# One forward substitution for four heads, and spilled keys and queries, in a delta-net mixer

## The chip, the cores and the metric

The kernel runs on one core of a Trainium2 chip. The time is the device time of that core in microseconds, from launch to the end. The time before is the median of three runs, 2939.25 us (2938.39 to 2943.58). One more execution was recorded by the hardware profiler; it took 2940.32 us, and its span from the first to the last instruction is 2938.6 us.

## The reference

The program is a trunk of two layers over 1024 tokens of width 1024 in float32. Layer 0 has a gated delta-net mixer, layer 1 a retention mixer, and each is followed by a gated feed-forward block with a short convolution and by layer norms. The change touches the mixer of layer 0 alone. What it computes, with 8 heads, head width 128 and chunks of 64 tokens, is:

```python
proj = h @ w_in
qkv, z, a, bt = jnp.split(proj, ...)
qkv = jax.nn.silu(causal_dwconv(qkv, conv_w))          # 24 tiles of 128 features: q, k, v of 8 heads
q = _l2norm(q) * dk ** -0.5 ; k = _l2norm(k)
g = -exp(a_log) * softplus(a + dt_bias) ; gc = cumsum(g) ; decay = exp(gc_i - gc_j), i >= j
kk = where(strict, (k * beta) @ k.T * decay, 0)
sol = triangular_solve(kk + eye, [v * beta, k * beta * exp(gc)])   # unit lower triangular, per chunk and head
qk = where(causal, q @ k.T * decay, 0)
# scan over chunks: v_new = u - w @ S ; o = (q e^g) @ S + qk @ v_new ; S = S e^g_last + k^T v_new
o = rms_norm(o) * norm_w * silu(z) ; return o @ w_out
```

## The kernel before, in words

The kernel cuts the 1024 tokens into 8 chunks of 128 (NCH = 8; the delta rule gives the same result for any length of chunk). A "feature tile" is one 128-feature slice of q, k or v for all 1024 tokens; the code numbers them 0 to 7 (queries), 8 to 15 (keys, `GH + h` or `K + h`), 16 to 23 (values, `2 * GH + h` or `V + h`). It is kept as two half tiles of 512 tokens each in the tag `qkv`, which has 20 slots, so ten of the 24 feature tiles can be there at one time.

The delta-net stage is written as a set of Python generators, and a small planner, `run(todo)` (line 732), decides the order. Each generator has a priority (lower goes first) and yields either a delay, or a list of events to wait for, or a condition. The planner holds an estimated clock `clk[0]` that advances by a cost per matmul, and events carry an estimated time (`emit(name, lat)`, with the latencies in the table `LAT`). Whenever a generator may go on, the one with the smallest priority number does. The planner runs when the program is built. What it fixes on the chip is the order of all instructions of TensorE: each matmul is tied to the one before it (`pq`, line 703). Semaphores, the order on the other engines and the choice of buffers are made by the tile framework. `take(tag, n)` and `give(tag, n)` are the planner's own count of free buffers in `free`.

The generators before the change are:

- `gates()` (priority -1): decay and beta of all heads.
- `filler(items)` (priority 9, so it runs when nothing else may): projections with convolution. An item `("c", ti)` makes feature tile `ti`: a weight load, 48 matmuls of 512 columns, the convolution `conv_half` (ScalarE and VectorE, line 480), and for queries a sum of squares (`ssq_late`). It needs one slot of `qkv` for each half. An item `("z", ti)` makes an output gate, again 48 matmuls, and stores it to DRAM (`zd`); it needs no `qkv` slot. After each item one step of background work is done (`bg_step`, modulation vectors of later blocks).
- `t_path(p)` (p + 0.3) for pair p of heads: the decay matrices (`decay`, GpSimd, TensorE, VectorE, then Exp on ScalarE and a store to `Ld`), the key products (lines 851 to 868), and the forward substitution of the 32x32 diagonal blocks (lines 874 to 892). For the substitution the blocks of both heads are copied into `X`, of whose 32 columns 16 hold something (8 chunks of two heads) and 16 are set to zero, transposed in blocks of 32x32, and then 31 steps follow one another on VectorE, each a multiplication (line 883) and a subtraction (line 885). Pair p begins when pair p - 1 has passed the event `T0`.
- `t_chain(p)` (p + 0.2): the inverse blocks of 32 are joined to the whole inverse `R` with small matmuls; `prep(p)` (p + 0.25): transposed values and keys; `dt_half(p, q4)`: query-key products with decay.
- `scan(p, h)` (p + 0.0 and p + 0.05): the scan over 8 chunks, two heads side by side. At chunks 3 and 7 it starts `tail`, which writes the output of half the tokens and gives three `qkv` slots back.

Other buffers that matter: `aux` (4, one decay matrix `U` each), `lane` (4), `auh` (8 half tiles, for `R` and the second half of the query-key products), and `xT` (2, unused in this stage before).

The forward substitution before is

```python
for j in range(31):
    dve.tensor_tensor(tv, bc(Y[:, j + 1:, j], nj), bm(T[:, j, 0:nj], ni), ALU.mult)
    ts_ = T[:, j + 1:, 0:nj]
    dve.tensor_tensor(ts_, ts_, tv, ALU.subtract)
    yield LAT["fs"]
```

and the order of the filler is given by hand in `items`.

## Time and profile before

| What | us |
|---|---|
| median of three runs | 2939.25 |
| profiled execution | 2940.32 |
| its span | 2938.6 |
| TensorE matmul busy | 2810.8 (96%) |
| VectorE busy | 2210.9 (75%) |
| ScalarE busy | 1316.6 (45%) |
| GpSimd busy | 500.1 (17%) |
| planned delta-net stage, first filler matmul to last scan step | about 82 to 648 |

In the profile "PE" is TensorE (matmuls), "PEld" its weight loads, "DVE" VectorE, "ACT" ScalarE, "POOL" GpSimd and "SP" the engine that issues most DMAs. A row of a group reads: line, engine, operation, tile written <- tiles read, shape, count, then busy time, mean duration in ns, and the idle time before it with what ended it. A row of a stretch reads: from:to and length, then for each engine its busy time and the number of its instructions, then the granted TensorE clock (1.00 is full), the busy share of the DMA engines and GB/s. Matmuls overlap, so the duration of one (about 0.39 us for 512 columns) is longer than the step from one to the next.

### The profile page before, as it was taken

How to read it: one execution, taken by the hardware profiler on the slowest of the kernel's cores; microseconds unless marked ns; L12 is line 12 of the kernel's file. 1: busy time of each engine (PE TensorE's matmuls, PEld its weight loads, DVE VectorE, ACT ScalarE, POOL GpSimd, SP SyncE). 2: the span in 40 equal slices, each digit the busy share in tenths (PEclk: the TensorE clock that was granted, in tenths of full speed). 3: DMA queues.
4: the chain of work that ended last, by engine and by line, in shares of the span. 5: the costliest groups of instructions: out<-in, count | busy, mean ns of one | idle time of the engine just before them, and what ended most of it. 6: DMA issues, size and time to landing. Idle time of an engine off the chain costs nothing. (4 is left out here: it accounts for less than half of the span.)

```text
span 2938.6 us, 38910 instructions
## 1 busy us (share of the span) xinstructions
PE 2810.8 (96%) x13594; PEld 2291.5 (78%) x13594; DVE 2210.9 (75%) x3976; ACT 1316.6 (45%) x2413; POOL 500.1 (17%) x517
## 2 busy tenths in 40 slices
PE   8998899999999999999999999999999999999997
PEld 6887777887778888887778877777777788888886
DVE  6878787757688888858686665566789777777779
ACT  4745564444544444545333333221344544444543
POOL 0312221100013332000000021422202022331201
PEclk9999999999999999999999999999999999999999
DMA  7231222344245655745333364655573254434853
GB/s 289 84 119 62 80 79 80 112 161 158 86 154 175 215 186 173 290 148 188 133 136 112 129 233 139 209 166 163 188 243 134 77 190 143 134 125 157 295 186 115
DMA packets 248277, 459.01 MB, mean 156 GB/s; under 512 B 23633, under 2 KB 77265, under 8 KB 248081
## 3 DMA queue, kind: packets, MB, share of 16 engines
q1 hardware_dynamic: 215680, 404.87, 41.5%
q10 hardware_dynamic: 29760, 43.00, 4.0%
q0 software_dynamic: 2640, 8.65, 0.8%
q8 instruction: 107, 1.75, 0.2%
q14 instruction: 90, 0.73, 0.1%
HBM read 343.71 MB, written 112.72 MB: 155 GB/s over the span
## 5 line engine op out<-in xcount | busy, mean ns | idle before, releaser
L714 PE MATMUL acc<-hT,wh 128*128 128x512 f32 x960 | 301.9, 396 | 0.0
L1527 PE MATMUL acc<-bb,ab 128*128 128x512 f32 x984 | 232.9, 394 | 11.6 <-DVE bb L90 10.2
L1527 PEld LDWEIGHTS acc<-bb,ab 128*128 128x128 f32 x984 | 184.0, 189 | 54.7 <-DVE bb L90 14.6
L1229 PE MATMUL acc<-T,wb 128*128 128x512 f32 x840 | 204.0, 392 | 7.6 <-DVE wb L90 7.5
L714 PEld LDWEIGHTS acc<-hT,wh 128*128 128x128 f32 x960 | 183.7, 191 | 34.7
L89 ACT ACTIVATE ab<-ar 128x512 fp32r<-128x512 f32 x210 | 130.3, 625 | 167.8 <-PE mm L303 50.1
L714 PE MATMUL acc<-hT,wl 128*128 128x512 f32 x480 | 202.5, 422 | 0.0
L411 POOL TENSOR_TENSOR xg<-xg,gb 128x512 f32<-128x512 f32 x48 | 63.5, 1324 | 781.3 <-DMA xg<-xs 477.3
L90 DVE TENSOR_TENSOR ab<-ar,ab 128x512 fp32r<-128x512 f32 x210 | 146.5, 703 | 61.1 <-ACT ab L89 61.1
L1229 PEld LDWEIGHTS acc<-T,wb 128*128 128x128 f32 x840 | 156.4, 188 | 46.0 <-DVE wb L90 12.3
L90 DVE TENSOR_TENSOR wl<-wr,wh 128x1024 fp32r<-128x1024 f32 x98 | 122.4, 1249 | 75.6 <-ACT wh L89 75.4
L1692 POOL TENSOR_TENSOR o<-o 128x512 f32<-128x512 f32 x80 | 126.5, 1592 | 279.6 <-PE acc L112 185.3
L90 DVE TENSOR_TENSOR wb<-wr,wb 128x512 fp32r<-128x512 f32 x162 | 117.0, 727 | 73.2 <-ACT wb L89 71.8
L89 ACT ACTIVATE wh<-wr 128x1024 fp32r<-128x1024 f32 x98 | 103.9, 1061 | 152.0 <-PE acc L714 65.0
L90 DVE TENSOR_TENSOR wb<-mm,wb 128x512 fp32r<-128x512 f32 x216 | 145.6, 683 | 26.4 <-ACT wb L89 25.6
L1661 DVE SCALAR_TENSOR_TENSOR o<-g,vc,o 128x512 f32<-128x512 f32 (+2 forms) x176 | 153.0, 887 | 6.7 <-ACT o L1656 6.1
L89 ACT ACTIVATE wb<-mm 128x512 fp32r<-128x512 f32 x216 | 124.2, 595 | 72.1 <-DVE mm L1283 65.1
L89 ACT ACTIVATE wb<-wr 128x512 fp32r<-128x512 f32 x162 | 98.5, 627 | 107.1 <-DMA wr<-in_ffn_up 50.6
L1299 ACT ACTIVATE pc<-acc 128x512 f32<-128x512 f32 x143 | 84.6, 591 | 137.8 <-PE acc L1229 88.3
L714 PE MATMUL acc<-wh,hT 128*128 128x512 f32 x384 | 135.5, 417 | 1.0 <-DVE vv L90 1.0
L490 DVE SCALAR_TENSOR_TENSOR qkv<-raw,vc,qkv 128x512 f32<-128x512 f32 x144 | 111.6, 778 | 14.7 <-ACT qkv L488 13.8
L110 PE MATMUL acc<-T,wb 128*128 128x512 f32 x292 | 115.3, 395 | 5.4 <-DVE wb L90 5.4
(651 smaller groups left out, 7450.5 us busy)
## 6 DMA issues: line engine op xcount, KB each, us to landing
wr<-in_ffn_up SPq DMA_DIRECT2D x92, 512.0 KB, 4.3
mvw<-in_ada_w SPq DMA_DIRECT2D x80, 512.0 KB, 4.6
ad<-o SPq DMA_DIRECT2D x154, 256.0 KB, 3.0
ar<-ad SPq DMA_DIRECT2D x154, 256.0 KB, 3.7
Br<-in_ffn_down SPq DMA_DIRECT2D x88, 256.0 KB, 3.3
wr<-in_ret_wv SPq DMA_DIRECT2D x32, 512.0 KB, 4.2
ar<-od SPq DMA_DIRECT2D x56, 256.0 KB, 5.3
wr<-in_gdn_wqkv SPq DMA_DIRECT2D x24, 512.0 KB, 3.6
```

The source lines that it names most:

```text
L89: act.activation(dst_h, src, AF.Copy)
L90: eng.tensor_tensor(dst_l, src, dst_h, ALU.subtract)
L110: mm(acc, wl[:, k], hl[0], start=first, stop=False)
L411: pool.tensor_tensor(x, x, gb[0], ALU.mult)
L490: dve.scalar_tensor_tensor(oh, raw[:, 3 - j:515 - j], w[:, 3 - j:4 - j], oh, ALU.mult, ALU.add)
L714: pq(pe.matmul(out, lhsT, rhs, start=start, stop=stop), cost)
L1229: return pe.matmul(*a, skip_group_check=True, **kw)
L1299: act.activation(t, X, AF.Copy)
L1527: return pe.matmul(*args, skip_group_check=True, **kw)
L1661: dve.scalar_tensor_tensor(tv, gv[:, c0 - j:c1 - j], w[:, 2 - j:3 - j], tv, ALU.mult, ALU.add)
L1692: (dve if fp == 0 else pool).tensor_tensor(o[d], o[x], o[y], op)
```

## The change

Four things are done together, all in the delta-net stage.

1. `t_path` now serves a group g of four heads (two pairs): all 32 columns of `X` are used, and there are two forward substitutions of 31 steps instead of four. The decay matrices move out into a generator of their own, `t_decay(h)`, one per head, in order; those of heads 4 to 7 wait for the first tails of pair 0 (event `("M", 0)`). The decay matrices of heads 4 and 5 live in `xT`, those of the others in `aux`. `t_chain(p)` of both pairs of a group reads its half of the columns of the shared result; `RX` and `TX` are given back by the second one.
2. The substitution yields to the planner after every third step, for 4.4 instead of 1.3 after each.
3. `filler` has two more kinds of work. While the next item needs `qkv` slots and fewer than two are free, it first makes one of the feature tiles in the list `[q2, q3, k4, k5, k6, k7]` in an `xT` buffer and stores it to a new DRAM tensor `qd` (kind `"s"`), if an `xT` buffer is free, and otherwise a gate (`"z"`). A tile that was put away is loaded from `qd` when its item comes up and two slots are free.
4. The hand-written order of items is new: keys 2 and 3 come before the values, and the gates are no longer in the list but taken when the filler is short of slots, or at the end.

```diff
--- before.py
+++ after.py
@@ -764,7 +764,7 @@
     def q4s(q4):
         return slice(q4 * 4, (q4 + 1) * 4)
 
-    free = {"qkv": 20 - 2 * (len(first) - 1), "lane": 4, "aux": 4, "auh": 8, "t2": 3}
+    free = {"qkv": 20 - 2 * (len(first) - 1), "lane": 4, "aux": 4, "auh": 8, "t2": 3, "xT": 2}
 
     def take(tag, n):
         while free[tag] < n:
@@ -827,21 +827,23 @@
             dve.tensor_tensor(U[h][:, q4s(q4)], v4(pt), bm(mneg, 4), ALU.add)
             give("t2", 2)
 
-    def t_path(p):
-        heads = pairs[p]
-        yield after_ev(("T0", p - 1), ("g",))
-        yield from take("lane", 1)
-        X = tl("lane", [P, 32, 32], name="X")
-        pool.memset(X[:, :, 16:32], 0.0)
-        for h in heads:
-            yield from take("aux", 1)
-            U[h] = tl("aux", [P, NCH, P], name="U")
-            yield from decay(h)
-        for h in heads:
-            act.activation(flat(U[h]), flat(U[h]), AF.Exp)
-            sp.dma_start(Ld[h], flat(U[h]))
+    def uhome(h):
+        return "xT" if h in (4, 5) else "aux"
+
+    def t_decay(h):
+        yield after_ev(("g",), ("DD", h - 1), ("M", h // 4 - 1))
+        yield from take(uhome(h), 1)
+        U[h] = tl(uhome(h), [P, NCH, P], name="U")
+        yield from decay(h)
+        act.activation(flat(U[h]), flat(U[h]), AF.Exp)
+        sp.dma_start(Ld[h], flat(U[h]))
+        emit(("DD", h))
+
+    def t_path(g):
+        heads = pairs[2 * g] + pairs[2 * g + 1]
+        X = None
         for hh, h in enumerate(heads):
-            yield after_ev(("f", GH + h))
+            yield after_ev(("f", GH + h), ("DD", h))
             sk = tl("sm", [P, NCH], name="sk")
             cj[h] = tl("sm", [P, NCH], name="cj")
             ir[h] = tl("sm", [P, NCH], name="ir")
@@ -866,6 +868,10 @@
                     n = q4 * 4 + c
                     dve.scalar_tensor_tensor(U[h][:, n], pt[:, c * P:(c + 1) * P], cj[h][:, n:n + 1],
                                              U[h][:, n], ALU.mult, ALU.mult)
+            if X is None:
+                yield after_ev(("T0", 2 * g - 1))
+                yield from take("lane", 1)
+                X = tl("lane", [P, 32, 32], name="X")
             for b in range(4):
                 bs = slice(32 * b, 32 * b + 32)
                 act.activation(X[bs, :, hh * 8:hh * 8 + 8].rearrange("p i c -> p c i"), U[h][bs, :, bs], AF.Copy)
@@ -883,17 +889,18 @@
             dve.tensor_tensor(tv, bc(Y[:, j + 1:, j], nj), bm(T[:, j, 0:nj], ni), ALU.mult)
             ts_ = T[:, j + 1:, 0:nj]
             dve.tensor_tensor(ts_, ts_, tv, ALU.subtract)
-            yield LAT["fs"]
+            if j % 3 == 2:
+                yield LAT["fs"]
         RX = tl("lane", [P, 32, 32], name="RX")
         dve.transpose(flat(RX), flat(T))
         TP = tl("lane", [P, 32, 32], name="TP")
         act.activation(TP, T.rearrange("p i j -> p j i"), AF.Copy)
         TX = tl("lane", [P, 32, 32], name="TX")
         dve.transpose(flat(TX), flat(TP))
-        RTX[p] = (RX, TX)
+        RTX[g] = (RX, TX)
         give("lane", 1)
-        emit(("Tq", p))
-        emit(("T", p), LAT["T"])
+        emit(("Tq", g))
+        emit(("T", g), LAT["T"])
 
     def rx(h, n):
         return R[h][n // 4][:, n % 4 * P:n % 4 * P + P]
@@ -903,15 +910,16 @@
 
     def t_chain(p):
         heads = pairs[p]
-        yield after_ev(("T", p), ("Dt", p - 1))
-        RX, TX = RTX[p]
+        yield after_ev(("T", p // 2), ("Dt", p - 1))
+        RX, TX = RTX[p // 2]
+        cx = p % 2 * 16
         yield from take("auh", 4)
         yield from take("lane", 1)
         emit(("T0", p))
         T0 = tl("lane", [P, 2, NCH, 64], name="T0")
         lo, hi = slice(0, 64), slice(64, 128)
         for hh, h in enumerate(heads):
-            ch = slice(hh * 8, hh * 8 + 8)
+            ch = slice(cx + hh * 8, cx + hh * 8 + 8)
             pool.memset(T0[0:32, hh, :, 32:64], 0.0)
             for b in range(3):
                 bs = slice(32 * b, 32 * b + 32)
@@ -922,7 +930,7 @@
             for q4 in range(2):
                 Rv = v4(R[h][q4])
                 pool.memset(Rv, 0.0)
-                ch = slice(hh * 8 + q4 * 4, hh * 8 + q4 * 4 + 4)
+                ch = slice(cx + hh * 8 + q4 * 4, cx + hh * 8 + q4 * 4 + 4)
                 for b in range(4):
                     bs = slice(32 * b, 32 * b + 32)
                     src = RX[bs, :, ch].rearrange("p i c -> p c i")
@@ -930,7 +938,8 @@
                         act.activation(Rv[bs, :, bs], src, AF.Copy)
                     else:
                         pool.tensor_copy(Rv[bs, :, bs], src)
-        give("lane", 2)
+        if cx:
+            give("lane", 2)
         yield LAT["T0"]
         yield from take("t2", 1)
         pa = mm_tile()
@@ -985,7 +994,7 @@
 
     def prep(p):
         heads = pairs[p]
-        yield after_ev(("Tq", p), *[("f", 2 * GH + h) for h in heads])
+        yield after_ev(("Tq", p // 2), *[("f", 2 * GH + h) for h in heads])
         for q4 in range(2):
             for h in heads:
                 pt = mm_tile()
@@ -1007,12 +1016,12 @@
     def dt_half(p, q4):
         heads = pairs[p]
         if q4 == 0:
-            yield after_ev(("Tq", p), ("M", p - 1))
+            yield after_ev(("Tq", p // 2), ("M", p - 1))
             yield from take("lane", 1)
             t = tl("lane", [P, 2, HALF], name="DT")
             tiles = [t[:, 0], t[:, 1]]
         else:
-            yield after_ev(("Tq", p), ("S", p - 1))
+            yield after_ev(("Tq", p // 2), ("S", p - 1))
             yield from take("auh", 2)
             emit(("Dt", p))
             tiles = [tl("auh", [P, HALF], name="DT") for _ in range(2)]
@@ -1076,7 +1085,7 @@
                 yield [(0.5, tail(p, h, n // 4))]
             if n < NCH - 1:
                 yield LAT["s3"]
-        give("aux", 1)
+        give(uhome(h), 1)
         emit(("Sh", h))
         if all(("Sh", g) in events for g in pairs[p]):
             emit(("S", p))
@@ -1119,10 +1128,31 @@
     def ssq_late(ti):
         yield LAT["ssq"]
         ssq_tile(ti, ptr)
-        emit(("f", ti), 1.0)
-
-    def filler(items):
-        for kind, ti in items:
+        if ti in away:
+            give("xT", 1)
+        else:
+            emit(("f", ti), 1.0)
+
+    qd = dr.tile([3 * GH, P, S], F32, tag="qd", name="qd")
+    away = []
+
+    def filler(items, zs, qs):
+        items = list(items)
+        while items or zs:
+            short = not items or (items[0][0] == "c" and free["qkv"] < 2)
+            if short and qs and items and free["xT"]:
+                kind, ti = "s", qs.pop(0)
+            elif short and zs:
+                kind, ti = "z", zs.pop(0)
+            else:
+                kind, ti = items.pop(0)
+            if kind == "c" and ti in away:
+                yield from take("qkv", 2)
+                feats[ti] = two("qkv", F32, "qkv")
+                for half in range(2):
+                    sp.dma_start(feats[ti][half], qd[ti, :, hs(half)])
+                emit(("f", ti), LAT["ld"])
+                continue
             if kind == "h":
                 if ti > 1:
                     acc = acc_tile()
@@ -1135,10 +1165,14 @@
                 else:
                     emit(("f", first[ti]), LAT["fv"])
                 continue
-            w = load_w(A["gdn_wqkv" if kind == "c" else "gdn_wz"][ti])
+            w = load_w(A["gdn_wz" if kind == "z" else "gdn_wqkv"][ti])
             prev = None
-            if kind == "c":
+            if kind != "z":
                 feats[ti] = []
+            if kind == "s":
+                yield from take("xT", 1)
+                away.append(ti)
+                oq = two("xT", F32, "oq")
             for half in range(2):
                 if kind == "c":
                     yield from take("qkv", 1)
@@ -1146,35 +1180,40 @@
                 for k in range(KT):
                     mm3(acc, w, k, hT[half][k], k == 0, k == KT - 1, pm)
                     yield 0.0
-                if kind == "c":
-                    feats[ti].append(tl("qkv", [P, HALF], name="qkv"))
+                if kind != "z":
+                    feats[ti].append(tl("qkv", [P, HALF], name="qkv") if kind == "c" else oq[half])
                     prev = conv_half(ti, acc, half, feats[ti], prev)
+                    if kind == "s":
+                        act.dma_start(qd[ti, :, hs(half)], feats[ti][half])
                 else:
                     cv = tl("cv", [P, 516], name="sg")
                     act.activation(cv[:, 0:HALF], acc, AF.Silu)
                     act.dma_start(zd[ti, :, hs(half)], cv[:, 0:HALF])
-            if kind == "c":
+            if kind != "z":
                 if ti < GH:
                     yield [(0.2, ssq_late(ti))]
+                elif kind == "s":
+                    give("xT", 1)
                 else:
                     emit(("f", ti), LAT["fv"])
             bg_step(acc_tile)
 
-    LAT = {"kk": 3.05, "ld": 1.14, "g1": 17.30, "gm": 2.50, "mm": 1.81, "T": 4.98, "X": 3.38, "fs": 1.3, "T0": 5.00, "t1": 1.65, "t2": 2.35, "t3": 1.34, "D": 2.67, "s1": 1.60, "s2": 1.22, "s3": 1.26, "tail": 12.31, "ssq": 9.30, "fv": 2.85}
+    LAT = {"kk": 3.05, "ld": 1.14, "g1": 17.30, "gm": 2.50, "mm": 1.81, "T": 4.98, "X": 3.38, "fs": 4.4, "T0": 5.00, "t1": 1.65, "t2": 2.35, "t3": 1.34, "D": 2.67, "s1": 1.60, "s2": 1.22, "s3": 1.26, "tail": 12.31, "ssq": 9.30, "fv": 2.85}
     pairs = [(2 * p, 2 * p + 1) for p in range(GH // 2)]
     for nm in ("S", "T0", "Dt", "M"):
         events[nm, -1] = 0.0
     events["Sh", -1] = events["Sh", -2] = 0.0
     c, z = "c", "z"
     K, V = GH, 2 * GH
-    items = [("h", 1), ("h", 2), ("h", 3), (c, 1), (c, V), (c, V + 1), (c, K + 2), (c, K + 3), (c, V + 2), (c, V + 3), (z, 0), (z, 1), (z, 2),
-             (c, 2), (c, 3), (c, K + 4), (c, K + 5), (c, V + 4), (c, V + 5),
-             (c, 4), (c, 5), (c, K + 6), (c, K + 7), (c, V + 6), (c, V + 7), (c, 6), (c, 7),
-             (z, 3), (z, 4), (z, 5), (z, 6), (z, 7)]
-    todo = [(-1.0, gates()), (9.0, filler(items))]
+    items = [("h", 1), ("h", 2), (c, K + 2), (c, K + 3), ("h", 3), (c, V), (c, V + 1), (c, 1), (c, V + 2), (c, V + 3),
+             (c, 2), (c, 3), (c, K + 4), (c, K + 5), (c, K + 6), (c, K + 7),
+             (c, V + 4), (c, V + 5), (c, 4), (c, 5), (c, V + 6), (c, V + 7), (c, 6), (c, 7)]
+    events["DD", -1] = 0.0
+    todo = [(-1.0, gates()), (9.0, filler(items, list(range(GH)), [2, 3, K + 4, K + 5, K + 6, K + 7]))] + [(h // 2 + 0.28, t_decay(h)) for h in range(GH)]
     for p in range(4):
-        todo += [(p + 0.3, t_path(p)), (p + 0.2, t_chain(p)), (p + 0.25, prep(p)), (p + 0.22, dt_half(p, 0)), (p + 0.24, dt_half(p, 1)),
+        todo += [(p + 0.2, t_chain(p)), (p + 0.25, prep(p)), (p + 0.22, dt_half(p, 0)), (p + 0.24, dt_half(p, 1)),
                  (p + 0.0, scan(p, pairs[p][0])), (p + 0.05, scan(p, pairs[p][1]))]
+    todo += [(2 * g + 0.3, t_path(g)) for g in range(2)]
     run(todo)
     zearly = list(range(GH))
```

## The prediction

> **What bounds the kernel now.** I read the page first, then the stretches of the delta-net stage, then the groups of TensorE and VectorE inside it, and last the waits. Outside the stage the change alters nothing, so the sum is made over the stage, 82 to 648 us of the span.
>
> ```profile
> span 2938.6 us, 38910 instructions
> 82.00:648.00 566.00, 529.47 (x3509) 448.80 (x3509) 425.86 (x1094) 303.59 (x658) 107.15 (x166) 0.96 0.29 95
> 142.00:191.00 49.00, 49.00 (x220) 40.58 (x219) 46.34 (x102) 20.06 (x39) 1.72 (x5) 1.00 0.30 95
> 245.00:277.00 32.00, 27.63 (x181) 23.91 (x180) 28.80 (x107) 18.14 (x44) 7.05 (x11) 1.00 0.05 17
> 551.00:600.00 49.00, 44.74 (x414) 38.06 (x413) 22.32 (x42) 20.71 (x54) 3.81 (x10) 0.93 0.32 105
> 600.00:648.00 48.00, 46.09 (x272) 40.01 (x271) 23.16 (x61) 20.60 (x44) 2.02 (x2) 1.00 0.49 162
> ```
>
> The columns after the length are busy time and count of PE, PEld, DVE, ACT and POOL, then the clock. PE looks busy for 529.47 of 566 us, but matmuls overlap, so the reader should count them. The first substitution lies in 142 to 191; there, with filler always at hand, PE did 216 wide matmuls in 48.81 us, 0.226 us each. That is its rate when nothing is late.
>
> ```profile
> 142.00:191.00 49.00, 48.81 (x216) 40.12 (x215) 1.00 0.30 95
> L714 PE MATMUL acc<-hT,wh 128*128 128x512 f32 x960 | 301.9, 396 | 0.0
> L714 PE MATMUL acc<-hT,wl 128*128 128x512 f32 x480 | 202.5, 422 | 0.0
> L714 PE MATMUL mm<-gm,m_lowr 128*128 128x512 f32 x32 | 10.7, 416 | 2.0 <-DVE qkv L994 1.9
> L714 PE MATMUL mm<-qkv 128*128 128x128 f32 x256 | 37.5, 297 | 7.8 <-DVE qkv L994 5.8 <-DVE U L867 2.1
> ...
> L714 PE MATMUL sc<-u,R 128*128 128x128 f32 x112 | 23.0, 289 | 1.6 <-DVE u L1052 1.5
> 246.23 1.06 PE L714 MATMUL mm<-qkv 128*128 128x128 f32 x8
> 214.87 2.11 PE L714 MATMUL mm<-T,U 32*32 32x32 f32 x64
> 226.64 2.08 PE L714 MATMUL mm<-T,U 64*64 64x64 f32 x32
> ```
>
> Work of PE in the stage: 1472 matmuls of 512 columns (960 and 480 of the filler, 32 of the decays) at 0.226 are 333 us. The groups of 128 columns, from mm<-qkv x256 down to sc<-u,R x112 and the smaller ones, count 1120; eight in a row took 1.06 us, so a step is (1.06 - 0.28) / 7 = 0.111 and they are 124 us. The 32- and 64-wide ones, at 2.11 / 64 and 2.08 / 32, add 34. Together 491 us. The stage lasts 566, so PE loses 75 us, and this is the most that any new order can win: 2940.3 - 75 = 2865.
>
> Where it is lost: in one hole of 40 us, and a little in each chain and scan.
>
> ```profile
> 226.00:265.80 39.80, 0.00 (x0) 0.00 (x0) 0.00 (x0) 0.00 (x0) 0.00 (x0) 0.91 0.18 64
> 226.00:265.80 39.80, 32.15 (x242) 27.92 (x243) 31.24 (x126) 19.56 (x42) 10.38 (x11) 0.91 0.18 64
> PE mm L714 <- DVE qkv L994: 10.0, 4, 4.1
> PE sc L714 <- ACT w L1057: 6.7, 7, 1.8
> ```
>
> The first row counts the instructions that touch the filler's input: none from 226 to 265.8, because all `qkv` slots are taken until the first tails. The second row is everything: 242 small matmuls, 64 of them 64-wide, worth 178 x 0.111 + 64 x 0.065 = 24 us. So this hole costs 16 us. The other 59 are the 4% of clock missing in the stage's row (0.96 of 566, 23 us, of which 3.6 in the hole) and waits of PE, which works in order, for results that came later than the planner thought; the two longest kinds are shown. With filler present they stay: 551 to 600 is the last chain, with gates to fill, and by the same count it still loses about 9 us; 600 to 648, a scan with gates, about 3.
>
> The chain of dependences is the other limit.
>
> ```profile
> 142.00:192.00 50.00, 10.53 (x31) 1.00 0.30 97
> 500.00:552.00 52.00, 10.47 (x31) 0.93 0.33 112
> 245.10:273.00 27.90, 4.77 (x14) 1.00 0.05 20
> 357.10:404.00 46.90, 4.69 (x14) 1.00 0.11 34
> 600.40:644.00 43.60, 4.89 (x14) 1.00 0.45 151
> L1098 ACT ACTIVATE DT<-mm,vc x4: 687/688/690, 265.6 to 290.0; 128x512 f32<-128x512 f32 x4
> L1098 ACT ACTIVATE DT<-mm,vc x4: 687/688/746, 391.0 to 420.8; 128x512 f32<-128x512 f32 x4
> ```
>
> The first two rows are the 31 multiplications of the first and the last substitution (line 883): each takes about 50 us, though its own multiplications are 10.5. The next three are line 1052 in the scans of pairs 0, 1 and 3. From the end of a substitution (191, 551) to the scan (245, 600) pass 49 to 54 us. The scan without filler is done in about 31 us, with filler in about 48. The last rows are the output copies of the tails of pairs 0 and 1: the first is out 20 us after its scan began without filler (245 to 266) and 34 us after one with it (357 to 391); with the second head I take 37. The last of pair 1 comes 64 us after its scan began (421).
>
> **The change part by part.** Durations are of the profiled execution, 2940.3 us; the median, 2939.25, is 1 us less, and I carry no correction.
>
> ```profile
> L490 DVE SCALAR_TENSOR_TENSOR qkv<-raw,vc,qkv 128x512 f32<-128x512 f32 x136 | 106.1, 780 | 12.5 <-ACT qkv L488 11.7
> L885 DVE TENSOR_TENSOR T<-T,fs 128x31 f32<-128x31 f32 (+15 forms) x124 | 42.1, 339 | 1.9
> L883 DVE TENSOR_TENSOR fs<-Y,T 128x31 f32<-128x31 f32 (+15 forms) x124 | 41.9, 338 | 1.7
> L90 DVE TENSOR_TENSOR wl<-wr,wh 128x1024 fp32r<-128x1024 f32 x31 | 38.0, 1227 | 2.9 <-ACT wh L89 2.7
> L239 DVE SCALAR_TENSOR_TENSOR ada<-mvw,e,ada 128x512 f32<-128x512 f32 x48 | 37.8, 787 | 7.9 <-DMA mvw<-in_ada_w 7.7
> L867 DVE SCALAR_TENSOR_TENSOR U<-mm,cj,U 128x128 f32<-128x128 f32 x64 | 18.0, 344 | 0.5
> L857 DVE SCALAR_TENSOR_TENSOR jk<-mm,cst 128x128 f32<-128x128 f32 x64 | 15.6, 301 | 5.6 <-PE mm L714 5.6
> L857 DVE DVE_READ_ACCUMULATOR jk<-mm,cst 128x1 f32 x64 | 5.8, 98 | 0.0
> L827 DVE TENSOR_TENSOR U<-mm,mneg 128x512 f32<-128x512 f32 x16 | 10.9, 681 | 7.0 <-PE mm L714 7.0
> L892 DVE STREAM_TRANSPOSE TX<-TP 128x1024 f32<-128x1024 f32 x4 | 5.0, 1243 | 3.3 <-ACT TP L890 3.3
> L841 ACT ACT_TABLE_LOAD x6 | 7.7, 1283 | 0.1
> zd<-sg ACTq DMA_DIRECT2D x16, 256.0 KB, 2.1
> zg<-zd SPq DMA_DIRECT2D x5, 512.0 KB, 3.8
> ```
>
> *Two substitutions instead of four.* VectorE loses 62 x (0.339 + 0.338) = 42 us and six transposes of 1.24, together 49 of its 426 us. No matmul goes, so by itself this moves PE's end by nothing; it shortens the queue in front of the results that PE waits for, and takes two 50 us pieces out of the chain.
>
> *When the first scan starts.* Two more heads have to be ready: for each, 8 x (0.301 + 0.098 + 0.344) and about 1 us of small operations and two decay additions of 0.68, some 8.3 us of VectorE, which is busy 46.34 of 49 us there. So 17 us later: substitution ends at 208 instead of 191, scan 0 at 208 + 54 = 262 with filler to 310, its first tails at 299, its last at about 325. Cover: convolutions and spills on PE go on meanwhile, so PE pays nothing.
>
> *Chain 1* needs four `auh` halves, which scan 0 gives at half time, 286; scan 1 at 286 + 48 = 334 (the last chain's 49, less the copies already made), to 382. *The second substitution* waits for the first tails (299), for keys 5 to 7 to be loaded after the last tails (325 + 4), for three heads of key products (about 8 each) and the copies (7): it starts near 360, ends near 412; scan 2 at 466 to 514; chain 3 beside it, scan 3 at 538 to about 580. That chain is 68 us shorter than now, but PE needs 491 us from 82 on and can't be done at 580 unless it loses only 7. So PE sets the end, and the chain has some 30 us of slack.
>
> *Spills.* Nothing is computed twice: each tile has its 48 matmuls once, earlier. By about 184 the seven tiles that fit into the free slots and the half one before them are done (7.5 units of 48 x 0.226 = 10.9 us, with 20 us of small work). Six spills (65 us) and eight gates (87), with the small work between, then cover PE past 371, when the tails of scan 1 free slots again. So the hole of 16 us is covered, and pays what the same stretch of a chain with filler does, 5 (551 to 600 loses 9 in 49, the hole is the later half of a chain and the start of a scan): minus 11.
>
> *The DMAs.* Twelve stores of 256 KB from ScalarE's queue (2.1 us like zd<-sg) and twelve loads on SP's (near zg<-zd's 3.8 for 512 KB); the planner reckons 1.14 after the load. Behind a load that waits for its slot stand SP's weight loads; the split of the next weights is what would be late. Three batches, between 0 and 4 us each: 0 to 12, I take 1, since the gates' weights are loaded a unit ahead.
>
> *Exp and Silu now alternate per head*, so up to four more table loads of 1.3 on ScalarE, busy 303.59 of 566: 0 to 5, I take 1. Copies of `RX`, one memset less and the yield after three steps: same instructions, nothing; if the bunches of six delay a scan's VectorE step by 2 us each they cost up to 10, and I keep that for the range.
>
> *The end.* Gates used up early no longer cover the last scan. A scan's 148 matmuls are 16 of its 31 us, so bare it loses 15, covered 3: between 0 and 12. About three gates should be left by my count, so 4.
>
> *Waits and clock,* the other 59: between 0 and 59 less. VectorE's load falls by 12%, no substitution of another pair runs inside scans 0, 2 and 3, and chains 1 and 3 run beside a scan and share its losses. I take a quarter, 15.
>
> Sum: -11 + 1 + 1 + 4 - 15 = -20, so **2920 us**.
>
> The granted clock is 0.91 in the hole and 0.93 from 551 to 600, but 1.00 in 245 to 277, which has no filler for most of its length. The Trainium skill, "TensorE: Matmul & The Clock Gate", Part 1, says that the clock is halved when the array has been idle for a while and comes back under steady work. By that rule a stage without holes would win nearly all 23 us of clock, and the sum would be about 2905; the 1.00 in the thinly filled scan agrees with it only in part.
>
> **The rivals.**
>
> *The losses nearly vanish* (0.16). Filler at every moment, clock at 1.00, results in time: PE loses 15 to 30 and the time is 2880 to 2895. For it: the 49 us at full rate in 142 to 191. Against: 551 to 600 has filler and still loses 9.
>
> *What is won is lost at the end* (0.13). Gates gone by 470, queries 6 and 7 held back until the tails of scan 2, last scan bare: 8 more for the scan and 10 for the pause before it, and the time is about 2938, no change. For it: the gates leave the list. Against: PE is behind the chain, so gates should be left.
>
> *Slower: the first substitution starves on VectorE* (0.17). From 121 each filler unit of 10.9 us brings 6 x 0.78 + 1.23 + 2 x 0.79 = 7.5 us of VectorE work, now without gates in between. If that always goes first, the 47 us of four heads' key products (25) and substitution (22) get 31% of the engine and end at 121 + 150 = 271 instead of 208. All later dates shift with them: 580 + 63 = 643, and with 15 more at the second one the end is 658, time 2950. It decides from an end at about 276. Against: in 142 to 191 VectorE is busy 46.34 of 49 us and the substitution still took 49.
>
> *PE has nothing to give* (inside my forecast's low end). Busy 529.47 of 566 would leave 36 us at most, 2904. The Trainium skill, "Perfetto Trace Analysis", Identifying the Most-Contended Engine, holds matmul busy time for no measure and takes that of the weight loads. With PEld at 448.80 of 566 it would allow 117 us and 2823; my count lies between the two and sides with neither.
>
> **How the numbers follow.** Forecast, a gain of 8 to 45 us: 0.54, own range 2895 to 2932. With the rivals' 0.16, 0.13 and 0.17 that makes 1. The range reaches from 2885, where a third of the first rival is left out, to 2946, where most of the starving one is: 0.05 and 0.11 outside. About 0.2% (6 us) is what runs of this kernel can tell. Faster 0.70 (forecast and first rival), same 0.12, slower 0.18.
>
> **What the changed profile would show.** Line 883 62 times, its first group starting near 157 and ending near 208; filler matmuls without a pause from 226 to 266; the second group near 360 to 412; last scan ending 620 to 635. VectorE down by about 49 us. PE's count of wide matmuls unchanged at 1472: more would mean that a tile was made twice. I am wrong if the first group ends past 250, if a new hole opens near 480, or if SP waits long in front of loads from `qd`.

## The result and the profile after

The changed kernel takes 2944.11 us, median of 20 runs (2935.63 to 2956.91); the kernel before takes 2939.38 us in as many (2934.70 to 2948.40). The ratio is 1.0013 (95%: 1.0002 to 1.0023): a little slower, by less than the 0.2% named in the prediction as the bound of what can be told from no change. The time lies 24 us above the predicted value, on the other side of the kernel before. It is outside the forecast's own range (2895 to 2932) and inside the widest one (2885 to 2946). That is luck: the upper end was there for the rival in which the first substitution starves on VectorE, and this is not what happened. The profiled execution took 2945.26 us.

First the stretches of the stage in the kernel after: length, busy time and count of PE, PEld, DVE, ACT and POOL, clock, DMA share, GB/s. Below the "..." are the same kind of rows for the instructions that touch the filler's input.

```profile
span 2943.5 us, 38792 instructions
82.00:648.00 566.00, 521.10 (x3503) 442.43 (x3503) 397.32 (x971) 302.82 (x660) 101.61 (x160) 0.97 0.33 108
82.00:169.00 87.00, 78.13 (x367) 64.46 (x367) 70.69 (x192) 62.57 (x98) 32.39 (x40) 0.96 0.24 80
169.00:219.00 50.00, 47.42 (x228) 38.80 (x226) 47.15 (x103) 20.64 (x52) 1.84 (x7) 1.00 0.33 104
226.00:265.80 39.80, 36.93 (x374) 31.55 (x374) 24.01 (x50) 23.62 (x73) 2.06 (x10) 0.95 0.32 100
551.00:600.00 49.00, 49.00 (x281) 42.36 (x280) 29.16 (x55) 23.44 (x76) 2.87 (x5) 1.00 0.56 178
584.00:638.00 54.00, 54.00 (x320) 47.26 (x319) 26.46 (x63) 21.64 (x60) 3.02 (x3) 1.00 0.54 183
...
82.00:169.00 87.00, 66.70 (x269) 51.50 (x269) 0.00 (x0) 0.00 (x0) 0.00 (x0) 0.96 0.24 80
226.00:265.80 39.80, 19.79 (x75) 13.34 (x75) 0.00 (x0) 0.00 (x0) 0.00 (x0) 0.95 0.32 100
```

The hole is filled: 75 wide filler matmuls from 226 to 265.8, where there were none. The last chain and the last scan are without a pause (49.00 of 49, 54.00 of 54). And yet PE is busy for 521.10 us of the stage, 8 less than before. Nor was work added: the whole program has 13594 matmuls, as before. What is new is the stretch ahead of the first substitution, 82 to 169, with PE idle for 9 us and a clock of 0.96.

The substitution and the spills, in rows of single lines (count, min/median/max ns, first and last start), and VectorE's groups:

```profile
L889 DVE TENSOR_TENSOR fs<-Y,T x62: 193/356/424, 169.2 to 458.4; 128x31 f32<-128x31 f32 x4, 128x60 f32<-128x60 f32 x4, 128x87 f32<-128x87 f32 x4, 128x112 f32<-128x112 f32 x4
L1187 ACTq DMA_DIRECT2D qd<-oq x12: 326/326/362, 207.2 to 353.4; - x12
L1153 SPq DMA_DIRECT2D qkv<-qd x12: 319/320/842, 278.6 to 358.6; - x12
```

```profile
L891 DVE TENSOR_TENSOR T<-T,fs 128x31 f32<-128x31 f32 (+15 forms) x62 | 21.0, 339 | 1.1
L889 DVE TENSOR_TENSOR fs<-Y,T 128x31 f32<-128x31 f32 (+15 forms) x62 | 21.0, 339 | 1.1
```

Line 889 (883 before) runs 62 times: 31 from 169 to 220 and 31 from 408 to 458. So two times 21.0 us of VectorE are gone, as forecast, and six transposes. The durations of all its instructions sum to 43 us less; its busy time, in which overlapping ones count once, fell by 29 (2210.9 to 2181.9). The stores of the spills are issued from 207 to 353, and the last load back at 359.

What PE waited for in the whole stage (total us, times, longest):

```profile
PE mm L714 <- DVE DT L1038: 12.2, 2, 7.0
PE mm L714 <- DVE U L827: 5.2, 2, 3.0
PE mm L714 <- DVE U L869: 3.5, 2, 2.6
...
PE sc L714 <- ACT w L1066: 2.7, 2, 1.9
```

The largest wait of before, 10.0 us for `qkv` of line 994, is down to 1.7 (line 1003 now), and that for `w` went from 6.7 to 2.7. New are two long waits until VectorE has read the first query-key product after each substitution (line 1038; before, such waits were 5.7 us in three places, the longest 2.5), and four in which a key product, or in one case a decay, waits for VectorE's decay addition (line 827) or key multiplication (line 869).

How much of the difference lies in the stage? The first transposes of the layer norm behind it, in the kernel before and then after:

```profile
L439 PE MATMUL mm<-cst,xt x96: 270/272/329, 758.2 to 2294.2; 128*128 128x128 f32 x96
```

```profile
L439 PE MATMUL mm<-cst,xt x96: 270/272/329, 759.9 to 2298.3; 128*128 128x128 f32 x96
```

They start 1.7 us later; the other 3 us between the two profiled executions arise behind it, where the kernels do the same. Over the profiled executions of this study the part behind that point took 2177 to 2189 us, though no edit touches it. So small differences are read from repeated times, not from one profile.

**Lost time, counted as in the prediction.** For each kernel, from its one profiled execution: the stretch less its matmuls at 0.2265 us (512 columns), 0.111 (128), 0.065 and 0.022 (64 and 32). It is split at the end of the first scan; "start" is from 82 to the first step of the substitution (in e3, e5, e6, e14 and e15 to the second, about 2.3 us later; up to the first they lose 1 us less). Times are medians; the ratio is to the kernel before on the same chip. The execution that was profiled can be up to 8 us off the median (e4: 2939.39 against 2947.40), so losses and medians in a row are not of the same execution.

| kernel | time us | ratio (95%) | start | to end of scan 0 | from there to 660 | lost in all |
|---|---|---|---|---|---|---|
| before | 2939.38 | | 2.1 | 21.6 | 53.8 | 75.4 |
| after | 2944.11 | 1.0013 (1.0002 to 1.0023) | 14.2 | 36.3 | 40.3 | 76.6 |
| e1_spill_only | 2943.62 | 1.0019 (1.0005 to 1.0032) | 1.4 | 14.1 | 60.1 | 74.2 |
| e2_no_spill | 2938.18 | 0.9996 (0.9987 to 1.0006) | 13.6 | 26.3 | 46.6 | 72.9 |
| e3_exp_late | 2933.95 | 0.9985 (0.9977 to 0.9994) | 7.3 | 28.2 | 36.8 | 65.0 |
| e4_fs_slow | 2947.40 | 1.0029 (1.0015 to 1.0044) | 11.2 | 28.8 | 49.5 | 78.3 |
| e5_exp_dt_late | 2937.88 | 1.0009 (0.9998 to 1.0019) | 7.4 | 36.2 | 35.6 | 71.8 |
| e6_exp_late_no_spill | 2949.78 | 1.0044 (1.0028 to 1.0061) | 7.6 | 19.3 | 63.8 | 83.1 |
| e7_dt_late | 2945.37 | 1.0032 (1.0019 to 1.0046) | 13.6 | 42.0 | 32.3 | 74.2 |
| e8_before_dt_late | 2947.24 | 1.0042 (1.0027 to 1.0058) | 0.6 | 19.5 | 60.3 | 79.8 |
| e9_before_half_fs | 2930.74 | 0.9966 (0.9954 to 0.9977) | 0.7 | 22.9 | 40.5 | 63.4 |
| e10_exp_4 | 2939.09 | 1.0000 (0.9990 to 1.0009) | 6.0 | 29.2 | 37.8 | 67.0 |
| e11_exp_65 | 2951.00 | 1.0044 (1.0032 to 1.0057) | 17.3 | 39.6 | 42.9 | 82.5 |
| e12_decays_first | 2941.79 | 1.0018 (1.0008 to 1.0028) | 7.0 | 34.8 | 41.0 | 75.8 |
| e13_decay_own_psum | 2935.84 | 0.9992 (0.9983 to 1.0001) | 7.9 | 32.5 | 40.2 | 72.7 |
| e14_own_psum_exp_late | 2938.95 | 0.9996 (0.9986 to 1.0007) | 3.9 | 26.3 | 42.5 | 68.8 |
| e15_keys_first | 2946.00 | 1.0024 (1.0014 to 1.0034) | 8.0 | 33.6 | 43.5 | 77.1 |
| e16_skip_second_fs | 2940.37 | 1.0008 (0.9998 to 1.0019) | 13.4 | 39.6 | 35.0 | 74.6 |

The first two rows are the result in short: after the first scan the new kernel wins 13.5 us, and before its end it loses 14.7.

### The profile page after: what moved, and what is told of

It is laid out like the page before. It is cut to its first block, busy times and chain, and to the rows that moved or that the text cites. A ratio compares the mean times of both kernels' runs of the same rounds, so it can differ in the third digit from the quotient of the medians.

```text
span 2943.5 us, 38792 instructions
## 1 busy us (share of the span) xinstructions
PE 2807.8 (95%) x13594; PEld 2289.2 (78%) x13594; DVE 2181.9 (74%) x3846; ACT 1315.2 (45%) x2413; POOL 477.4 (16%) x509
## 4 chain that ended last, share of the span: by engine, by line
PE 61%; DVE 20%; DMA 9%; ACT 4%; issue 4%; POOL 1%; SPq 0%; DVEq 0%; ACTq 0%; POOLq 0%
PE acc L714 16%; PE acc L1268 6%; PE sc L714 4%; PE acc L110 4%; PE acc L111 4%; PE acc L112 4%; PE acc L1566 3%; PE sc L1268 3%; DVE o L1700 3%; DMA wr<-in_ffn_up 3%; DVE wb L90 3%; PE mm L714 2%; DMA mvw<-in_ada_w 2%; DVE mm L1322 1%; PE sc L110 1%
## 5 line engine op out<-in xcount | busy, mean ns | idle before, releaser
L1566 PEld LDWEIGHTS acc<-bb,ab 128*128 128x128 f32 x984 | 184.4, 190 | 56.2 <-DVE bb L90 15.7
L411 POOL TENSOR_TENSOR xg<-xg,gb 128x512 f32<-128x512 f32 x48 | 62.8, 1311 | 775.4 <-DMA xg<-xs 469.9
L90 DVE TENSOR_TENSOR wb<-wr,wb 128x512 fp32r<-128x512 f32 x162 | 116.6, 724 | 72.7 <-ACT wb L89 72.5
L89 ACT ACTIVATE wb<-mm 128x512 fp32r<-128x512 f32 x216 | 124.3, 595 | 75.8 <-DVE mm L1322 72.7
L1731 POOL TENSOR_TENSOR o<-o 128x512 f32<-128x512 f32 x80 | 111.5, 1403 | 285.9 <-DVE o L1723 104.5
L89 ACT ACTIVATE wb<-wr 128x512 fp32r<-128x512 f32 x162 | 98.6, 627 | 104.1 <-DMA wr<-in_ffn_up 46.6
L239 DVE SCALAR_TENSOR_TENSOR ada<-mvw,e,ada 128x512 f32<-128x512 f32 x140 | 106.5, 761 | 14.4 <-DMA mvw<-in_ada_w 13.8
```

Of the source, the lines that this page charges most:

```text
L89: act.activation(dst_h, src, AF.Copy)
L90: eng.tensor_tensor(dst_l, src, dst_h, ALU.subtract)
L239: dve.scalar_tensor_tensor(a, wr[:, kk], e[:, k:k + 1], a, ALU.mult, ALU.add)
L1566: return pe.matmul(*args, skip_group_check=True, **kw)
L1731: (dve if fp == 0 else pool).tensor_tensor(o[d], o[x], o[y], op)
```

## The experiments

**The parts, one at a time.** The prediction's gain had two sources, the filler in the hole and the freed VectorE. e1 does the first alone; e2 does the second with nothing put away (gates still fill where slots are short, and the longer decay and key stage comes with it); and e3 lets the planner order the key products later.

e1: the kernel before, with the new filler.

```diff
-    def filler(items):
-        for kind, ti in items:
+    def filler(items, zs, qs):      # as in the change: spills, then gates, while slots are short
...
-    todo = [(-1.0, gates()), (9.0, filler(items))]
+    todo = [(-1.0, gates()), (9.0, filler(items, list(range(GH)), [2, 3, K + 4, K + 5, K + 6, K + 7]))]
```

> The kernel before with the new filler alone: gates and put-away tiles fill while slots are short; substitutions stay at two heads each, in the old order. If the loss of the change sits in the four-head path (theory A: decays, key products and substitution of four heads make TensorE wait), then the hole at 226 to 266 closes, nothing new opens, and the time is 2920 to 2932. If parking tiles in DRAM and pulling the convolutions forward is what costs (theory B: VectorE crowded in the first 220 us, loads from DRAM late), it is 2940 to 2950.

Four of the six tiles were put away here. 2943.62 us, 1.0019 (1.0005 to 1.0032): the gain that theory A expected is not there. The first chain and scan lose 7.5 us less than in the kernel before, and everything later 6.3 more: the tails and the last scan have no gates left beside them. The row of 600 to 648, with PE busy for 46.09 of 48 us before the change:

```profile
600.00:648.00 48.00, 40.49 (x420) 34.55 (x418) 30.76 (x86) 19.55 (x48) 3.32 (x4) 0.96 0.36 129
```

Here the chain is as long as before, and the filler that was moved into one hole left another behind.

e2: the kernel after, nothing put away.

```diff
-    ... filler(items, list(range(GH)), [2, 3, K + 4, K + 5, K + 6, K + 7]))]
+    ... filler(items, list(range(GH)), []))]
```

> The changed kernel with an empty list of tiles to put away: only gates fill while slots are short, keys 4 to 7 are made when slots come free. Theory A: the losses of TensorE before 220 us stay, the second substitution starts later because four keys still have to be made, 2945 to 2965. Theory B: with less convolution work beside the first substitution it gets faster, 2930 to 2940.

2938.18, 0.9996 (0.9987 to 1.0006): as fast as before. Here gates alone fill the stretches without slots, and still the start loses 13.6. PE's order is that of the kernel after up to 228 us, and the first spill is stored at 207: that loss has nothing to do with the spills.

e3: the kernel after; the planner reckons with 5 us for a head's exponentials, so that it orders its key products later.

```diff
-        emit(("DD", h))
+        emit(("DD", h), 5.0)
```

> The changed kernel, but the planner reckons 5 us from the last decay addition of a head to the moment its key products may be ordered; no instruction is added or removed. Theory A (a key product is put before Exp is done and then holds one of the two PSUM tiles of its kind, so the next decay waits): the loss of TensorE between 116 and 142 us falls from 10 to about 3, time 2935 to 2940. Theory B: VectorE is crowded there anyway, nothing moves, 2942 to 2947.

2933.95, 0.9985 (0.9977 to 0.9994): faster than both kernels. The start, all instructions and then the waits:

```profile
82.00:177.00 95.00, 91.00 (x436) 75.27 (x435) 75.88 (x198) 66.16 (x115) 32.19 (x41) 0.98 0.27 89
```

```profile
PE mm L714 <- DVE U L827: 3.0, 2, 2.4
PE acc L714 <- DVE wl L90: 0.7, 1, 0.7
PE mm L714 <- DVE U L869: 0.4, 1, 0.4
```

Half of the loss is gone (14.2 to 7.3), and so are 4.6 of the 8.7 us of waits there. Against the kernel after the time fell by 8 (by the ratios) to 10 us (by the medians).

**What exactly is waited for.** Matmuls write their results into PSUM tiles, and the next matmul that needs a tile must wait until its content has been read. Decays (read by line 827) and key products (read by line 869) share two such tiles, `mm`. In the kernel before, the decays of both heads stand ahead of the first key product. In the kernel after, they alternate from 111 us on: PE starts decays at 111.07, 116.97, 124.64, 129.46, 133.55 and 141.35, and key products at 114.57, 122.65, 129.92 and 137.50. So each waits until VectorE has read what the other kind left in the tile. e13 gives the decays of the first four heads tiles of their own, those that the scans use later; e12 puts all four decays ahead of the key products; e10 and e11 vary the 5 us; e14 joins e13 and e3.

```diff
-            pt = mm_tile()                      # in decay(h)
+            pt = sc_tile() if h < 4 else mm_tile()
```

> The changed kernel with the decays of heads 0 to 3 in the PSUM tiles of the scans (free until the first scan) instead of the two that key products, transposes and products share. Theory A, in its sharper form (a decay whose addition VectorE does late holds one of two PSUM tiles, and the next key product on TensorE waits): loss before the first substitution falls from 14 to 3 to 6, time 2932 to 2939. If TensorE waits there for VectorE in another way, the loss stays above 10 and the time at 2941 to 2947.

2935.84, 0.9992 (0.9983 to 1.0001), 6 to 8 us less than the kernel after, and a start that loses 7.9 instead of 14.2 (e2, e7 and e16, which have the order and the tiles of the kernel after there, lose 13.4 to 13.6). PE's order in the trace is that of the kernel after and only the tiles were changed, so the shared tiles are shown to be a cause. What is left of the waits there:

```profile
PE sc L714 <- DVE U L827: 2.3, 1, 2.3
PE mm L714 <- DVE U L869: 1.8, 1, 1.8
```

The expected loss of 3 to 6 was missed (the time, 2932 to 2939, was not): VectorE (67 us busy in those 79) is late for the decays themselves too.

```diff
-            yield after_ev(("f", GH + h), ("DD", h))
+            yield after_ev(("f", GH + h), ("DD", heads[-1]))
```

> The changed kernel with all four decays of a group ordered before its first key product, as the kernel before has it for two heads. Theory A: loss before the first substitution falls from 14 to below 7, the first substitution starts 5 to 15 us later, time 2930 to 2940. If instead VectorE's crowd sets that loss, it stays near 14, and the time is 2944 to 2955.

2941.79, 1.0018 (1.0008 to 1.0028). The start loses 7.0 here too, so the alternation is part of the cause. But the substitution starts at 183, 14 us later than in the kernel after, and from there to the end of scan 0 27.8 us are lost instead of 22.1. This takes back most of what the start gave.

For e10 and e11 the edit is that of e3 with 4.0 and 6.5 in place of 5.0.

> The changed kernel with 4 us after Exp instead of 5. Theory A (the order around Exp costs TensorE 7 to 11 us before the first substitution): nearly the gain of 5 us, 2932 to 2939, and a loss of 6 to 9 us before the first substitution. Theory D (any small shift of the plan scatters the time by 10 us, and the 5 us were lucky): 2940 to 2950, or a gain that does not come from the stretch before the first substitution.

> The changed kernel with 6.5 us after Exp. Theory A: 2930 to 2939, loss before the first substitution 3 to 8 us. Theory D: anything from 2930 to 2950, with no relation to that stretch.

e10: 2939.09, 1.0000 (0.9990 to 1.0009), start 6.0. e11: 2951.00, 1.0044 (1.0032 to 1.0057), start 17.3, against the expectation. In e11 one kind of wait has grown, and the first substitution begins at 198:

```profile
PE mm L714 <- DVE U L827: 9.9, 3, 4.2
```

So the estimate of 5 us is no measured latency that the planner should be told; it shifts an order, and which filler, decay and key product then meet on VectorE seems to decide. e10 has a better start than e3, and its median is 5 us longer. The profiled executions don't show these 5 us: the layer norm behind the stage begins at 746.4 in e10 and at 746.9 in e3, both 13 us ahead of the kernel after.

> The same with the 5 us after Exp. Theory A: both mend the same loss, so no more than the 5 us alone, 2931 to 2937. Theory D (small shifts of the plan scatter the time): 2937 to 2950.

2938.95, 0.9996 (0.9986 to 1.0007), in the order of e3 (up to 646 us in the trace). The start is the best of all with four heads (3.9), but the two gains don't add up: the stretches after scan 0 lose 42.5 instead of e3's 36.8.

**Do the long waits after the substitution matter?** The kernel after waits 5.2 and 7.0 us for a tile `mm` that holds one of the first query-key products, until VectorE reads it (line 1038). These products are ordered before the decays that they are multiplied with can be loaded, since the load waits for the slot that the substitution holds. e4 makes the planner reckon with a slower substitution; e7 orders these products later; e5 does so together with e3's edit; e8 does it in the kernel before.

```diff
-           "fs": 4.4
+           "fs": 5.0
```

> The changed kernel, but three steps of the substitution are reckoned at 5.0 instead of 4.4 us, 50 instead of 44 in all, as the trace has them. Theory A (query-key products and transposes of the chain are put ahead of the substitution's real end, TensorE waits 5.2 and 7.0 us for them): these two waits shrink below 2 us each, time 2934 to 2940. Theory B: what the substitution's neighbours lose is VectorE time, no change, 2942 to 2947.

```diff
-        yield LAT["ld"]
+        yield 6.5 if q4 == 0 else LAT["ld"]
```

> The changed kernel with the later query-key products alone. Theory A: minus 8 to 12 us against the changed kernel, 2932 to 2937. Theory C: 2941 to 2947.

> The changed kernel with the 5 us after Exp and, besides, the first query-key products of a pair reckoned 6.5 us after their decays are asked for instead of 1.14 (the buffer of those decays comes free only with the copy after the substitution, and the load takes 3 us). Theory A (TensorE loses by orders that come too early): the two waits of 5 to 7 us at the start of chains 0 and 2 go, time 2922 to 2930. Theory C (the loss only moves to the next late result in the chain): 2931 to 2936, as with the 5 us alone.

> The kernel before with the later query-key products. Its waits for these products are 5.7 us in three places. Theory A says this loss was there before the change too: 2932 to 2937. If only the four-head order suffers from it: 2937 to 2942.

None gained: e4 2947.40, 1.0029 (1.0015 to 1.0044); e7 2945.37, 1.0032 (1.0019 to 1.0046); e5 2937.88, 1.0009 (0.9998 to 1.0019), 4 above e3; e8 1.0042 (1.0027 to 1.0058). In e5 the wait on line 1038 is gone, and the next results of the chain are late in its place, in the stretch 235 to 280, which loses 16.5 us:

```profile
PE mm L714 <- ACT T L927: 4.5, 2, 3.7
PE mm L717 <- DVE R L991: 0.9, 1, 0.9
```

In e4 the waits on line 1038 behind the two substitutions sum to 6.3 instead of 12.2, and the stretch from 314 to 346 newly loses 15. In these kernels a wait that was ordered away came back at a later step.

**What the freed VectorE is worth.** e9 takes it out of the kernel before, which then leaves out the steps of the second and the fourth substitution. e16 takes more of it out of the kernel after, all steps of the second substitution.

```diff
+            if p % 2 == 0:      # e9, in before; e16, in after: if g == 0
                 dve.tensor_tensor(tv, bc(Y[:, j + 1:, j], nj), bm(T[:, j, 0:nj], ni), ALU.mult)
                 ts_ = T[:, j + 1:, 0:nj]
                 dve.tensor_tensor(ts_, ts_, tv, ALU.subtract)
```

> The kernel before with the 31 steps of the substitution left out for pairs 1 and 3 (so two heads of each four get a wrong inverse); the planner keeps the time for them, so the order of TensorE is the same. It takes the same 42 us from VectorE as the change does. If a lighter VectorE shortens what TensorE waits for, as the forecast had it (15 us of waits), the time is 2922 to 2932. If the waits come from the planned order alone, 2936 to 2941.

> The changed kernel with the 31 steps of the second substitution left out (heads 4 to 7 get a wrong inverse), the plan unchanged. In the kernel before, 42 us less on VectorE gave 8 us. If VectorE still stands in the way, 21 us less gives 2 to 6: 2938 to 2942. If not, 2942 to 2946.

e9: 2930.74 (2927.75 to 2931.78), 0.9966 (0.9954 to 0.9977), with the planned order as it was. That is 8 us less than the kernel before on the same chip, the median of which was 2938.75. The whole stage of e9:

```profile
82.00:648.00 566.00, 531.82 (x3567) 449.13 (x3566) 403.96 (x988) 307.65 (x666) 111.55 (x166) 0.99 0.31 100
```

The clock is 0.99 here and 0.96 in the kernel before. All of the gain lies behind scan 0 (40.5 us lost instead of 53.8). One thing e9 does not tell apart: without the steps, VectorE has less to do, and what depends on them is also ready some 50 us earlier. e16: 2940.37, 1.0008 (0.9998 to 1.0019), at most 4 us for another 21 us of VectorE, and the interval overlaps that of the kernel after: with two substitutions gone, no gain from the third is shown.

**Is parking the keys and queries worth anything?** The runs disagree. e6 is e3 with nothing put away (both edits shown); e15 is e3 with the keys of heads 4 to 7 put away, and asked for, ahead of queries 2 and 3.

> The changed kernel with the 5 us after Exp and nothing put away in DRAM. If parking tiles is worth something once the first losses are gone, this is slower than the 2934 with parking: 2936 to 2945. If parking is worth nothing or costs, 2926 to 2934.

> The changed kernel with the 5 us after Exp, and keys 4 to 7 put away and asked for ahead of queries 2 and 3. The second substitution should start 10 to 25 us earlier than 406. If the chain of dependences sets the end, the time falls by as much, 2915 to 2925. If TensorE's work does (it is without loss in the last 80 us before the last scan), the time stays at 2930 to 2938, or rises because the queries come late.

e6: 2949.78, 1.0044 (1.0028 to 1.0061), 16 us slower than e3; the stretches after scan 0 lose 63.8, the last two scans among them 26. e15: 2946.00, 1.0024 (1.0014 to 1.0034). The second substitution starts at 400 instead of 406, no more, and the second scan only at 392 instead of 335, since its queries come last.

So with e3's edit, parking seems worth 16 us. Without it the same comparison says the opposite: e2, which puts nothing away, is 5 us (by the ratios) faster than the kernel after. What parking is worth by itself is not settled.

## Why the prediction was wrong, point by point

**"PE pays nothing" for two more heads (priced 0, costs 12 us): the step that failed.** The prediction moved the first scan 17 us later and said that convolutions and spills go on meanwhile. They do, but PE works in order, and the decays and key products stand between them. In the kernel before, the same stretch of 61 us, all, then filler, then decays:

```profile
82.00:143.00 61.00, 61.00 (x290) 50.97 (x290) 48.51 (x122) 46.96 (x92) 22.38 (x31) 0.97 0.30 95
...
82.00:143.00 61.00, 55.29 (x228) 43.14 (x228) 0.00 (x0) 0.00 (x0) 0.00 (x0) 0.97 0.30 95
...
82.00:143.00 61.00, 2.57 (x8) 1.42 (x8) 13.07 (x11) 0.97 0.30 95
```

236 wide matmuls at 0.2265 and 54 at 0.111 are 59.4 us: 1.6 lost (2.1 with the few narrow ones at their own step). After: 269 of the filler, 16 of the decays and 82 others are 73.7 of 87: 13.3 lost (14.2). Before, the third and fourth head's decays and key products were spread over the chain behind the first substitution. Now those of all four heads stand ahead of the first substitution, and decays and key products alternate. VectorE as a whole is not busier for it. The stretch in which most is lost, first before and then after the change:

```profile
116.00:142.00 26.00, 26.00 (x136) 22.19 (x135) 24.01 (x79) 19.85 (x41) 9.00 (x16) 1.00 0.32 106
...
116.00:142.00 26.00, 19.53 (x82) 15.51 (x81) 21.52 (x73) 16.18 (x20) 13.68 (x15) 0.87 0.28 102
```

VectorE had 24.01 us of work there before, and PE did not pause; after, it has 21.52, and PE pauses for 6.5. PE's instructions after the change show it (start, us, instruction, idle time before it):

```profile
122.65 1.16 PE L714 MATMUL mm<-qkv 128*128 128x128 f32 x8 [3.01 <-DVE U L827]
...
137.50 1.49 PE L714 MATMUL mm<-qkv 128*128 128x128 f32 x8 [2.64 <-DVE U L869]
138.65 0.77 PE L714 MATMUL acc<-hT,wl 128*128 128x512 f32 x1
139.22 1.05 PE L714 MATMUL acc<-hT,wh 128*128 128x512 f32 x2
140.07 0.63 PE L714 MATMUL acc<-hT,wl 128*128 128x512 f32 x1
```

The key products wait for a PSUM tile that VectorE has not read yet, and behind them stands all filler. After the second of these waits the clock is at half: from 139.22 to 140.07 two wide matmuls take 0.85, 0.425 each instead of 0.2265. The four waits are 8.7 us, and the two stretches of half clock (3.4 us each; one is in the last section) cost about 3 more. e13 and e3 show the cause from two sides: with other tiles, or another order, 6 to 7 us of the 12 go, and the time falls by 6 to 10. With both (e14) 10 of the 12 go, though the time falls by only 5.

The rival "the first substitution starves on VectorE" named the right engine and the wrong victim. It was to decide from an end at 276, and the substitution ended at 220. The substitution came 12 us later than forecast (169 to 220 against 157 to 208) and took no longer; PE lost the time, in waiting for tiles.

**The hole (-11): filled, but little of it won.** In the very stretch of 226 to 265.8 PE now loses 6.9 us instead of 15.7. But the chain and scan as a whole, 190 to 272 before and 220 to 316 after, lose 19.5 and 18.1: what the filler gives there, the 5.2 us wait on line 1038 and the half clock behind it take back. e1 shows also what filler in a hole is worth when the chain is as long as it was: nothing.

**The freed VectorE (-15): about half the size.** e9 gives 8 us in time and 12 in lost time, and the 12 are clock, not shorter waits (last section). Of the change's own rows, the 13.5 us won after the first scan may be of this kind: e9 wins 13.3 there without a new order. The prediction's "a quarter" of 59 was a guess without a row behind it.

**The dates.** First scan 266 to 316 (forecast 262 to 310), first tails from 301 (299), second scan 332 to 381 (334 to 382): right within 6 us. The second substitution, 408 to 458, comes 48 us later than forecast. The prediction let the spills run in one piece, and end near 250 (184 plus 65); they ended at 353. The planner does them only where nothing else is ready and an `xT` buffer is free, and the last keys were back at 359, with three heads of key products still to do. The last scan ends at 637; the chain alone was to allow 580, and PE's work 620 to 635. (The "some 30 us of slack" between the two should have been 40 to 55.) The late second substitution cost nothing that could be found: the last scans had filler to the end (54.00 of 54). An earlier second substitution (e15), or none in the same order (e16), won nothing that is clear of the noise.

**The end (+4), DMAs (+1), table loads (+1).** No scan was bare at the end (0.7 lost in the last one; the gates lasted). ScalarE has two table loads more, 2.6 us. What the loads from `qd` did in SP's queue (total us, times, longest):

```profile
SPq L1153 <- DMA qd<-oq: 19.7, 3, 10.2
```

Three of them waited for their own stores, up to 10.2 us, and no wait of PE is put down to them.

**Sum.** Forecast -20: hole -11, VectorE and clock -15, the rest +6. Found: about -1 for the first chain and scan, -13.5 behind it (VectorE, clock and the covered end together), +12 at the start, and +4 in the first substitution, which lost nothing before (three waits of 0.8 to 0.9 us there, for transposed values and query-key products, are 2.5 of it). That is about +1, and the profiled stage is 1.7 us longer.

**What stays open.** The medians differ by 4.7 us and the profiled stages by 1.7; where the rest arises was not found. The +4 in the first substitution is explained for 2.5 us only. Nor is it settled why 4.0, 5.0 and 6.5 us in one line give 2939, 2934 and 2951: small shifts of the order moved the time by 5 to 15 us, and part of e3's gain may be such luck. That the start can be mended is shown by three edits of different kinds (e3, e12, e13); that e3's size of gain belongs to the mend alone is not.

## What to carry to other kernels

Count a stretch's matmuls times their undisturbed step: the difference to its length is all that an order can win, and it shows at once where a change loses. When more heads are joined into one step, look at what must exist before that step: the work that used to be spread out is now in one place, and in-order PE waits for whichever PSUM tile its readers free last. Filler that was moved into a hole was no gain here while the chain behind the hole stayed as long; the hole came back where the filler had been.

## What the runs showed of the hardware

Short waits can cost more than their length. The granted clock in the kernel after, first beside a wait of 2.18 us (until 114.57), then behind waits of 2.64 (until 137.50), 6.95 (464.88) and 2.14 us (484.34):

```profile
112.00:121.00 9.00, 5.46 (x27) 3.93 (x25) 7.83 (x17) 6.27 (x7) 4.89 (x4) 1.00 0.41 147
138.00:142.00 4.00, 4.00 (x15) 3.34 (x15) 2.62 (x16) 0.35 (x1) 1.65 (x1) 0.57 0.00 0
462.00:469.00 7.00, 4.12 (x16) 3.83 (x17) 2.72 (x5) 6.81 (x14) 3.58 (x10) 0.53 0.21 72
486.00:490.00 4.00, 4.00 (x25) 3.15 (x24) 1.39 (x2) 3.59 (x7) 0.56 (x2) 0.57 0.01 2
```

The clock fell after a wait of 2.14 us and not after one of 2.18, so the length of the one wait doesn't decide alone. What helps is where it falls. In all 18 traces the clock changes only on a grid of steps of 3.41 us. The wait of 2.64 us lies within one step (134.75 to 138.16), and the clock falls at that step's end. The wait of 2.18 us is divided by the end of a step at 114.27, with 1.89 us in the one and 0.29 in the next, and the clock stays. Over the stages of all traces (82 to 660 us), every one of the 72 steps at full clock in which PE was idle for more than 1.95 us (by the profile's busy times) was followed by half clock. Of the other 2459, 30 were followed by it, 14 of these with matmuls of 32 or 64 columns in them, as behind the wait of 2.14 us; what decides there is open.

The Trainium skill, "TensorE: Matmul & The Clock Gate", Part 1, puts the idle window that leads to half clock at about 3.4 us. The steps in these traces have that length, but it was enough that PE was idle for some 2 us of one.

In the trace's clock records the stage before the change, from 82 up to the layer norm, has 47.7 us at half clock, with 19.8 us of PE's work in them, which take about twice their time. After the change it is 37.5 us with 17.0, and in e9 17.1 with 7.8. So the 12 us that e9 loses less are all clock (19.8 - 7.8); the rest of its lost time is what it was (62.8 and 62.9). The pauses of PE are about as long in sum, and fewer of them bring the clock down. In the kernel after the rest is 67.0, and in e13, with as much half clock (17.0), it is 63.0: what the shared tiles cost over the stage is waits. Each of these is one profiled execution, so how much of it is chance is open.
